# Last block of a hybrid RWKV-7 / attention layer: output rows loaded from the middle of the last gate, merge weights in pairs, raw first products, late load of x

## The chip, the cores and the metric

The kernel runs on one core of a Trainium2 chip. The time is device microseconds (us) of one execution. A core has TensorE (PE in the profile), VectorE (DVE), ScalarE (ACT), GpSimd (POOL), and SyncE (SP), which issues most of the DMAs.

## The reference, cut to what matters

One layer works on 640 tokens of width 1024 (512 latent and 128 context tokens). What the change touches is the end of the mixing part and the step behind it:

```python
u_rw, u_na, gate_rw, gate_na = jnp.split(h @ p["w_in"], IN_SPLITS, axis=-1)
o_rw, s_new = _rwkv_branch(u_rw, s0, ...)      # 8 heads of 64, a scan over the tokens in both directions
o_na = _na_latent(q, k, v, ctx_k, ctx_v, ...)  # 2-D neighbourhood attention, 8 heads of 64
merged = (jax.nn.sigmoid(gate_rw) * (o_rw @ p["w_o_rwkv"])
          + jax.nn.sigmoid(gate_na) * (o_na @ p["w_o_na"]))
x = x + g1 * (merged @ p["w_out"])
h2 = _rmsnorm(x, p["norm2_g"]) * (1.0 + sc2) + sh2
x = x + g2 * ((jax.nn.silu(h2 @ p["ffn_w1"]) * (h2 @ p["ffn_w3"])) @ p["ffn_w2"])
```

## The kernel before, in words

All tensors are float32. A product is made of three matmuls: each operand is split into a high part that the matmul takes exactly and a remainder (`split`, L185 on ACT and L186 on DVE or POOL), and hi·hi, hi·lo and lo·hi are added in PSUM. Weights are loaded 512 KB at a time into a buffer `wst` (`wdma`, L163, DMA on SP) and split by `wcast`: either ACT writes the high part (L173) and DVE subtracts (L175), or ACT writes the negated weight (L171) and an accumulating DMA that POOL issues adds the weight (L172). There are two buffers each for `wst` and for the split halves.

Attention comes first. Its output, split, is written to DRAM as `o_d`, rows 0 to 511. Then come four RWKV blocks, ct = 0 to 3, of two heads each. A block has a main part; `inv`, 30 steps on DVE that invert triangular matrices (L1250, L1254), ended by two transposes (L1263, L1265) and copies into `Rt` (L1284, L1295); `carry`, 8 sequential steps that pass a state through PE, ACT (L1327), PE, ACT (L1357), PE and DVE (L1376, tile `ZV`); and `out`, the group norm, bonus and gate (L1396 to L1412), which is spread over the next block. Three PE jobs of each block (L1145, L1148, L1173, L1185, L1196) stand at chosen steps of `inv`. Block ct = 3 leaves its output split in SBUF as `o3`.

Beside these chains runs a stream of weight units, taken in the order that the table `PRM` lists: projections (k, r, v, l), 16 gates (g0 to g15, `gate_gen`) and 16 merge units (a0 to a7: output rows 0 to 511 times `w_o`, gated with `gate_na`; b0 to b7: rows 512 to 895, gated with `gate_rw`). Their matmuls are L197 (`feat_gen`), with two PSUM buffers `fl` of 320 columns. `PRM["plan"]` gives how many of the stream's matmuls follow each step of a block. On PE, POOL, DVE and ACT the instructions of the blocks run in the order in which the code writes them; on SP a scheduler sets the order, and behind the blocks it sets that of DVE, ACT and POOL too.

The end of the stream, around which the change lies, goes like this. The last gate, g14, reads the layer's normed input `h`, whose SBUF the split output `o` takes over. So `o_load(0, 6)` (L1436, 12 DMAs of 320 KB) stands behind g14; a0 is the first reader. Each a unit (24 matmuls) loads its gate into a buffer `mx` (L1450), and DVE multiplies the PSUM result by the gate into a tile `mt` (L1464). Each b unit (18 matmuls) does the same (L1464) and adds to `mt` (L1467). Behind the blocks, `last_gen` multiplies `o3` by the last 128 rows of `w_o`: 8 chunks in two halves, 48 matmuls (L1576), each half gated (L1577), added to `mt` (L1579) and split (L1580 on ACT, L1581 on POOL). The product with `w_out` (`tok_gen`, L284; five token blocks, first 512 columns and then the other 512) is woven between. Its sums are gated with `G` (L1558) and added to `x2` (L1559), the reloaded x; that frees a PSUM bank for the other 512 columns. Loads of x (L1548, 5 of 512 KB) and G (L1553, 2 of 512 KB) go out before `last_gen`. Transposes of a small row (L1615, L1617) stand on PE between the two halves of the `w_out` product. Norm and feed-forward follow (L1718 and L284).

## Time and profile before

| | |
|---|---|
| median of 3 runs | 1191.83 us (1191.1 to 1192.4) |
| profiled execution, its own time | 1191.72 us |
| its span, first to last instruction | 1189.7 us |
| mean granted TensorE clock | 0.985 |
| PE busy | 1124.1 us (94% of the span) |
| DVE, ACT, POOL busy | 777.5, 530.5, 205.1 us |

A row of a timeline gives the start in us from the start of the span, the duration, the engine, the line, the operation and tiles, and how many instructions are joined; brackets give the idle time before it and what ended that. A window's columns are the busy us (and instructions) of PE, PE's weight loads, DVE, ACT and POOL, then the granted TensorE clock, the DMA engines' busy share and GB/s. A list of waits has the total, the count and the longest wait.

### The profile page before, as it was taken

The numbers are of one execution on the slowest core, as the hardware profiler recorded it, in microseconds if no ns is written. First come the engines' busy times: TensorE is split into PE (matmuls) and PEld (weight loads), VectorE is DVE, ScalarE is ACT, GpSimd is POOL, SyncE is SP. The second block draws the span as 40 slices with busy tenths as digits, with TensorE's granted clock in tenths as the row PEclk, the third lists the DMA queues.
The fourth block names the chain that finished last, engine by engine and source line by source line (L and its number), as shares of the span: only waits on it lengthen the run. The fifth ranks groups of instructions, "written<-read, shape, count | busy, mean of one in ns | idle before, by whom it ended". The sixth has DMA issues, their size and how long they took to land.

```text
span 1189.7 us, 26921 instructions
## 1 busy us (share of the span) xinstructions
PE 1124.1 (94%) x11160; PEld 998.3 (84%) x11160; DVE 777.5 (65%) x1630; ACT 530.5 (45%) x1053; POOL 205.1 (17%) x273
## 2 busy tenths in 40 slices
PE   6999999999999999999599799989999999999998
PEld 4688877789888988888488678889899989998997
DVE  4564455559469658836474675888568757775675
ACT  4444666554564664565133342654224422442340
POOL 1162244320111211111101250100001000000000
PEclk9999999999999999999799999999999999999999
DMA  9762767553333514433654851312312231232122
GB/s 335 265 117 84 244 216 230 191 146 98 103 93 84 153 50 104 123 93 79 200 138 110 245 218 54 107 49 79 104 57 86 89 107 54 89 100 90 59 75 103
DMA packets 61906, 149.42 MB, mean 126 GB/s; under 512 B 7732, under 2 KB 23732, under 8 KB 61784
## 3 DMA queue, kind: packets, MB, share of 16 engines
q1 hardware_dynamic: 55592, 131.56, 33.6%
q0 software_dynamic: 5328, 14.94, 6.8%
q8 instruction: 88, 1.44, 0.5%
q10 hardware_dynamic: 864, 1.20, 0.3%
q14 instruction: 34, 0.28, 0.1%
HBM read 118.41 MB, written 14.32 MB: 112 GB/s over the span
## 4 chain that ended last, share of the span: by engine, by line
PE 65%; DVE 8%; ACT 3%; DMA 2%; issue 1%; SPq 0%; ACTq 0%; DVEq 0%; POOLq 0%
PE f L1718 23%; PE acc L284 17%; PE fl L197 13%; DMA wlo<-wst 1%; DVE pr L1250 1%; PE w L1324 1%; PE w L1351 1%; DVE RL L1254 1%; PE mm L197 1%; PE w L1364 1%; PE w L1336 1%; PE w L1148 1%; DMA o<-o_d 1%; PE w L1196 1%; PE w L1126 1%
## 5 line engine op out<-in xcount | busy, mean ns | idle before, releaser
L1718 PE MATMUL f<-t,whi 128*128 128x320 f32 x640 | 141.4, 309 | 0.0
L1718 PE MATMUL f<-b,whi 128*128 128x320 f32 x608 | 136.5, 312 | 3.6 <-ACT b L185 1.8
L284 PE MATMUL acc<-whi,u 128*128 128x512 f32 (+1 forms) x448 | 136.0, 385 | 0.0
L197 PE MATMUL fl<-h,whi 128*128 128x320 f32 x704 | 126.5, 319 | 0.8 <-issue 0.8
L197 PEld LDWEIGHTS fl<-h,whi 128*128 128x128 f32 x704 | 106.1, 188 | 5.6 <-issue 0.9
L173 ACT CAST whi<-wst 128x1024 fp32r<-128x1024 f32 (+2 forms) x86 | 81.5, 953 | 64.7 <-PE acc L284 32.5
L1718 PEld LDWEIGHTS f<-t,whi 128*128 128x128 f32 x640 | 107.1, 188 | 0.0
L1718 PEld LDWEIGHTS f<-b,whi 128*128 128x128 f32 x608 | 103.0, 190 | 4.8 <-ACT b L185 2.2
L1718 PE MATMUL f<-t,wlo 128*128 128x320 f32 x320 | 98.9, 309 | 0.0
L284 PEld LDWEIGHTS acc<-whi,u 128*128 128x128 f32 x448 | 83.5, 188 | 16.7
L1718 PE MATMUL f<-b,wlo 128*128 128x320 f32 x304 | 94.7, 312 | 1.4 <-DVE wlo L1762 1.4
L1759 ACT CAST whi<-ws 128x1024 fp32r<-128x1024 f32 x40 | 42.0, 1051 | 108.7 <-PE f L1718 48.5
L1773 POOL TENSOR_TENSOR ws<-wst 128x512 f32<-128x512 f32 x20 | 28.2, 1409 | 341.3 <-DVE wlo L1762 226.7
L175 DVE TENSOR_TENSOR wlo<-wst,whi 128x1024 fp32r<-128x1024 f32 (+1 forms) x49 | 62.0, 1274 | 37.2 <-ACT whi L173 36.6
L284 PE MATMUL acc<-wlo,u 128*128 128x512 f32 (+1 forms) x224 | 86.3, 385 | 0.0
L284 PE MATMUL acc<-whi,h 128*128 128x512 f32 x240 | 78.0, 399 | 1.2 <-DVE h L398 1.1
L172 POOL DMA_DIRECT2D wlo<-wst x37 | 32.6, 881 | 232.4 <-ACT wlo L171 212.9
L1558 DVE SCALAR_TENSOR_TENSOR tt<-acc,G 128x512 f32<-128x512 f32 (+1 forms) x51 | 34.7, 681 | 50.5 <-PE acc L284 50.5
L197 PE MATMUL fl<-h,wlo 128*128 128x320 f32 x352 | 66.5, 321 | 0.0
L197 PE MATMUL fl<-o,whi 128*128 128x320 f32 x224 | 46.3, 337 | 16.8 <-DMA o<-o_d 10.0
L1759 ACT CAST whi<-wst 128x1024 fp32r<-128x1024 f32 (+1 forms) x48 | 41.3, 869 | 42.3 <-PE acc L284 37.6
L1718 PEld LDWEIGHTS f<-t,wlo 128*128 128x128 f32 x320 | 60.1, 188 | 0.0
(333 smaller groups left out, 2539.1 us busy)
## 6 DMA issues: line engine op xcount, KB each, us to landing
wst<-in_w_dram SPq DMA_DIRECT2D x66, 512.0 KB
wst<-in_w_rw_dram SPq DMA_DIRECT2D x31, 512.0 KB
wa<-in_w_ada_dram SPq DMA_DIRECT2D x24, 512.0 KB
wlo<-wst POOLq DMA_DIRECT2D x22, 512.0 KB, 4.5
f<-in_w_ada_dram SPq DMA_DIRECT2D x16, 512.0 KB
wst<-in_w_qkv_dram SPq DMA_DIRECT2D x12, 512.0 KB
o<-o_d SPq DMA_DIRECT2D x14, 320.0 KB
x<-in_xs_dram SPq DMA_DIRECT2D x8, 512.0 KB
```

Of the source, the lines that this page charges most:

```text
L172: pool.dma_start(lo[:, :n].bitcast(F32), st[:, :n], accum_op=ALU.add)
L173: act.copy(hi[:, :n], st[:, :n])
L175: dve.tensor_tensor(out=lo[:, :n], in0=st[:, :n], in1=hi[:, :n].bitcast(F32), op=ALU.subtract)
L197: pe.matmul(ps[:, :t1 - t0], w[:, a:a + 128], x[:, k0 + kt, t0:t1], start=n == 0, stop=n == 3 * nk - 1)
L284: pe.matmul(pss[i][:, a:b], lhs(x, kt, ts_), w[:, cs_], start=ki == 0 and n == 0, stop=ki == last and n == 2)
L1126: pe.matmul(t[r0:r0 + 32, 64 * i:64 * i + 64], S.BK[l // 10][own, l % 10, 0, 32 * bk:32 * bk + 32], V(AG[own, l, h, :], [[0, 2], [1, 32]], ...
L1148: pe.matmul(pr[h][hrows[h ^ i], o_], x[hrows[h], :], R_[hrows[h], l, :], start=True, stop=True)
L1196: pe.matmul(pt[h][hrows[h ^ i], o_], S.BK[l // 10][hrows[h], l % 10, i, :], idh(h), start=True, stop=True)
L1558: dve.scalar_tensor_tensor(out=tt, in0=ps[:, a:b], scalar=c, in1=G[:, g, sl], op0=ALU.mult, op1=ALU.mult)
L1718: pe.matmul(ps[:, :H2], w_[:, c_], x_[:, kt, :], start=first and kt + n == 0, stop=last and kt == 3 and n == 2, skip_group_check=more)
L1759: act.copy(r[0][:, :width], src())
L1773: eng_x(PRM["se"][i - 1]).tensor_tensor(out=o_, in0=x, in1=y, op=op)
```

## The change

Five things are changed, all in the last block and behind it.

1. The tiles that hold `h`, then `o`, then the merged sum, are cut in two halves of four row groups. The last gate is computed by a new `gate2_gen`: four row groups of both column halves, then the other four. After the first four, the first half of `h` has been read, and `o_load(0, 4)` is issued there; `o_load(4, 6)` follows where `o_load(0, 6)` stood.
2. Merge units are made in pairs: four a units of 48 matmuls (512 KB of weights each) and four b units of 36 (384 KB each). The four a units are split with POOL's DMA, the b units on DVE.
3. The a products go to `mt` raw, copied from PSUM by ACT (L1516 of the new text, where DVE's L1464 stood). A generator `gate_a` runs beside the last carry: it loads the gates (L1535) and DVE multiplies them in (L1545).
4. The last 128 rows of `w_o` are loaded into `wos` (L1599) and split (L189 on ACT, L190 on DVE) in step 0 of the last carry, no longer behind the blocks. The low part of `o3` is made by DVE, not POOL. The plan of block 3 gives a carry step 6 + 4 stream matmuls in place of 8 + 6, and has more of them in `inv`. Of the three PE jobs in `inv`, the second stands at step 8, before at step 11.
5. The pool for `x2` and `G` is opened behind the first half of the `w_out` product and takes memory that block 3 and `last_gen` used; loads of x (L1673) and G (L1678) come there. L1683 and L1684 are the former L1558 and L1559.

PE has as many instructions as before (8267 in the program's order); DVE has 1638 (1633), ACT 1009 (1012), POOL 266 (279), SP 371 (379).

SP around the loads of `o`; `wst` are pairs or single units of `w_o`, `tna_d` the gates' DRAM buffer, `o_d_80` the high and `o_d_81` the low parts. Before:

```order
L163 DMA wst_7543<-in_w_o_dram 128x512 [waits DMAHW6_49,DMAHW4_49,DMASW5_49]
L544 DMA tna_d<-fl_7413 128x320 [waits DMAHW5_49,Activation_49]
L163 DMA wst_7723<-in_w_o_dram 128x512 [waits DMAHW2_49,DMASW6_49,Activation_49]
L544 DMA tna_d<-fl_7545 128x320 [waits DMAHW7_49,Activation_49]
L1436 DMA o_7710<-o_d_81 128x640 [waits DMAHW0_49,PE_49]
L1436 DMA o_7710<-o_d_81 128x640 [waits DMAHW1_49]
L1436 DMA o_7710<-o_d_81 128x640
L1436 DMA o_7710<-o_d_81 128x640 [waits DMAHW3_49]
L1436 DMA o_7710<-o_d_81 128x640 [waits DMAHW4_49]
L1436 DMA o_7710<-o_d_81 128x640 [waits DMAHW5_49]
L1436 DMA o_7709<-o_d_80 128x640 [waits DMAHW6_49,PE_49]
L1436 DMA o_7709<-o_d_80 128x640 [waits DMAHW7_49]
```

The same place of the change:

```order
L164 DMA wst_7545<-in_w_o_dram 128x2x512 [waits DMAHW6_49,DMAHW4_49,DMASW5_49]
L559 DMA tna_d<-fl_7415 128x320 [waits DMAHW5_49,Activation_49]
L164 DMA wst_7721<-in_w_o_dram 128x2x512 [waits DMAHW2_49,DMASW6_49,Activation_49]
L1476 DMA o_7598<-o_d_81 128x640 [waits DMAHW7_49,PE_49]
L1476 DMA o_7596<-o_d_80 128x640 [waits DMAHW0_49,PE_49]
L1476 DMA o_7596<-o_d_80 128x640 [waits DMAHW1_49]
L1476 DMA o_7598<-o_d_81 128x640
L1476 DMA o_7596<-o_d_80 128x640 [waits DMAHW3_49]
L1476 DMA o_7598<-o_d_81 128x640 [waits DMAHW4_49]
L1476 DMA o_7596<-o_d_80 128x640 [waits DMAHW5_49]
L1476 DMA o_7598<-o_d_81 128x640 [waits DMAHW6_49]
```

High and low parts now alternate, and the four row groups of an a unit come first; a load of `w_o` that waits for POOL's DMA (DMASW6) still stands ahead of them.

DVE at the start of the last carry; `Rt` ends `inv`, `ZV` is the step's last operation. Before:

```order
L1295 COPY Rt<-w_8352 32x10x32 [waits Activation_49]
L1295 COPY Rt<-w_8353 32x10x32 [waits Activation_49]
L1464 SCALAR_TENSOR_TENSOR P_1091_8264<-mx_8221,fl_8334 128x320 [waits PE_49]
L1464 SCALAR_TENSOR_TENSOR kk_8402<-mx_8273,fl_8403 128x320 [waits DMAHW3_49,PE_49]
L1376 TENSOR_TENSOR ZV<-w_8429,Dt_6865 64x2x64 [waits PE_49]
L1376 TENSOR_TENSOR ZV<-w_8429,Dt_6865 64x2x64 x3
L1464 SCALAR_TENSOR_TENSOR kk_8402<-mx_8273,fl_8453 128x320 [waits PE_49]
L1376 TENSOR_TENSOR ZV<-w_8506,Dt_6865 64x2x64 [waits PE_49]
```

The change:

```order
L1333 COPY Rt<-w_8360 32x10x32 [waits Activation_49]
L1333 COPY Rt<-w_8361 32x10x32 [waits Activation_49]
L190 TENSOR_TENSOR f_1105_8468<-wos_8410,f_1104_8467 128x1024 [waits DMAHW1_49,DVE_49,Activation_49]
L1414 TENSOR_TENSOR ZV<-w_8437,Dt_6867 64x2x64 [waits PE_49]
L1414 TENSOR_TENSOR ZV<-w_8437,Dt_6867 64x2x64 x3
L1545 SCALAR_TENSOR_TENSOR mt_7723<-pre_8496,mt_7723 128x320 x2
L1545 SCALAR_TENSOR_TENSOR mt_7926<-pre_8498,mt_7926 128x320 [waits DMAHW7_49]
L1545 SCALAR_TENSOR_TENSOR mt_7926<-pre_8498,mt_7926 128x320
L1545 SCALAR_TENSOR_TENSOR mt_7977<-pre_8500,mt_7977 128x320 [waits DMAHW0_49]
L1545 SCALAR_TENSOR_TENSOR mt_7977<-pre_8500,mt_7977 128x320
L1414 TENSOR_TENSOR ZV<-w_8521,Dt_6867 64x2x64 [waits PE_49]
```

The subtraction of the last `w_o` rows now stands ahead of the first `ZV`, and six gatings stand between the first and the second.

DVE between the two halves of the `w_out` product; `acc` are the PSUM sums, `pc` the small transposes that PE makes behind the whole first half. Before:

```order
L175 TENSOR_TENSOR wlo_9379<-wst_9376,whi_9378 128x1024 [waits DVE_49,DMAHW2_49,PE_49,Activation_49]
L1558 SCALAR_TENSOR_TENSOR tt_9463<-acc_9189,G 128x512 [waits DMAHW7_49,PE_49,Pool_49]
L1559 TENSOR_TENSOR x_0_9087<-x_0_9087,tt_9463 128x512 [waits DVE_49]
L1558 SCALAR_TENSOR_TENSOR tt_9466<-acc_9190,G 128x512 [waits PE_49]
L1559 TENSOR_TENSOR x_1_9088<-x_1_9088,tt_9466 128x512 [waits DVE_49]
L1558 SCALAR_TENSOR_TENSOR tt_9469<-acc_9191,G 128x512 [waits PE_49]
L1559 TENSOR_TENSOR x_2_9089<-x_2_9089,tt_9469 128x512 [waits DVE_49]
L1558 SCALAR_TENSOR_TENSOR tt_9472<-acc_9192,G 128x512 [waits PE_49]
L1559 TENSOR_TENSOR x_3_9090<-x_3_9090,tt_9472 128x512 [waits DVE_49]
L1558 SCALAR_TENSOR_TENSOR tt_9475<-acc_9193,G 128x512 [waits DMAHW0_49,PE_49]
L1619 COPY s_9094<-pc_9439 128x16 [waits PE_49]
```

The change:

```order
L179 TENSOR_TENSOR wlo_9325<-wst_9322,whi_9324 128x1024 [waits DMAHW4_49,PE_49,Activation_49]
L1706 COPY s_9373<-pc_9402 128x16 [waits DVE_49,PE_49]
L1707 TENSOR_SCALAR m_9372<-pc_9402 128x16
L1708 TENSOR_TENSOR m_9372<-m_9372,C 128x16 [waits DVE_49]
L1683 SCALAR_TENSOR_TENSOR tt_9426<-acc_9135,G 128x512 [waits DMAHW4_49,Pool_49]
L1683 SCALAR_TENSOR_TENSOR tt_9429<-acc_9136,G 128x512
L1684 TENSOR_TENSOR x_0_9366<-x_0_9366,tt_9426 128x512 [waits DMAHW7_49,DVE_49]
L1684 TENSOR_TENSOR x_1_9367<-x_1_9367,tt_9429 128x512 [waits DMAHW0_49,DVE_49]
L1683 SCALAR_TENSOR_TENSOR tt_9432<-acc_9137,G 128x512 [waits DVE_49]
L1683 SCALAR_TENSOR_TENSOR tt_9435<-acc_9138,G 128x512 [waits DVE_49]
L1684 TENSOR_TENSOR x_2_9368<-x_2_9368,tt_9432 128x512 [waits DMAHW1_49,DVE_49]
```

The copy of `pc`, which waits for PE's transposes, now stands ahead of all the gated adds.

The core of the diff:

```diff
-     "0.0.0 16.1.0 8.1.1 9.0.0 2.1.0 8.1.1 8.1.1 ... 10.0 0.0 8.1 6.2 0.0 8.1 4.2 ..." (block 3 of the plan)
+     "0.0.0 16.1.0 8.1.1 9.0.0 2.1.0 8.1.1 13.1.1 ... 10.0 0.0 6.1 4.2 0.0 6.1 4.2 ..."
...
+    def gate2_gen(i, w, ps_, gsb, gtag):
+        ps = [ps_(), None]
+        for kts in ((0, 1), (2, 3), (4, 5), (6, 7)):
+            for hf, (a, b) in enumerate(halves):
+                if ps[hf] is None:
+                    ps[hf] = ps_()
+                for kt in kts:
+                    for n, (u, x) in enumerate(((w[0], hh), (w[0], hl), (w[1], hh))):
+                        pe.matmul(ps[hf][:, :H2], u[:, kt * 128:kt * 128 + 128], x[:, kt, a:b],
+                                  start=kt == 0 and n == 0, stop=kt == 7 and n == 2)
+                        yield
+            if kts[1] == 3:
+                o_load(0, 4)
...
-                        o_load(0, 6)
+                        o_load(4, 6)
...
-            k0, k1, src = (0, 4, tna_d) if g == "a" else (4, 7, trw_d)
-            return wdma(w_o[i][:, 128 * k0:128 * k1]), src[i]
+            k0, k1 = (0, 4) if g == "a" else (4, 7)
+            return wdma(w_o[2 * i:2 * i + 2, :, 128 * k0:128 * k1].rearrange("c p n -> p c n"))
...
+                        if g == "a":
+                            act.copy(mt[c8][:, a:b], ps[:, :b - a])
+                            copied.add((c8, a))
+                            return
...
+        def gate_a():
+            ts = []
+            def load():
+                if len(ts) < 8:
+                    ts.append(pre_t())
+                    sp.dma_start(ts[-1], tna_d[len(ts) - 1])
+            for _ in range(3):
+                load()
+            yield 0, 0
+            for c8 in range(8):
+                load()
+                for (a, b) in halves:
+                    while (c8, a) not in copied:
+                        yield 9, 9
+                    dve.scalar_tensor_tensor(out=mt[c8][:, a:b], in0=ts[c8][:, a:b], scalar=1.0, in1=mt[c8][:, a:b],
+                                             op0=ALU.add, op1=ALU.mult)
+                    yield 0, 0.45
...
-                    pg = iter(())
+                    pg = gate_a()
+                    wos = nk_t("wos", [P, 1280])
+                    sp.dma_start(V(wos[:, :], [[128, 8], [1, 128]]), w_o[:, :, 896:1024].rearrange("c p n -> p c n"))
+                    def wo_cast():
+                        wo.extend(f5()[:, 0:1024].bitcast(F32R) for _ in range(2))
+                        split(wo[0], wo[1], wos[:, 0:1024])
+                    later(wo_cast, (0.95, 1.1), 12)
...
-    wo = wload(w_o[:, :, 896:1024].rearrange("c p n -> p c n"))
...
-    nstack.close()
-    xpool = open_pool(ctx, "xpool")
...
     hs.close()
+    nstack.close()
+    xpool = open_pool(ctx, "xpool")
```

172 lines of the change are left out of this document (102 added, 70 removed).

## Prediction

> **What bounds the kernel now.** First the page: PE's busy share. Then PE's waits and the windows of the last block, to see where PE is not busy. Then the timelines of the engines waited for.
>
> ```profile
> PE 1124.1 (94%) x11160; PEld 998.3 (84%) x11160; DVE 777.5 (65%) x1630; ACT 530.5 (45%) x1053; POOL 205.1 (17%) x273
> ```
>
> ```profile
> 570.00:580.00 10.00, 6.07 (x21) 5.12 (x22) 2.08 (x8) 0.92 (x1) 0.00 (x0) 0.50 0.82 287
> 660.00:670.00 10.00, 8.41 (x55) 7.59 (x55) 4.97 (x11) 4.00 (x10) 3.79 (x4) 1.00 0.94 260
> 670.00:680.00 10.00, 6.56 (x38) 5.76 (x38) 6.74 (x12) 3.52 (x5) 2.47 (x2) 0.99 0.79 233
> 680.00:690.00 10.00, 9.62 (x39) 8.70 (x40) 10.00 (x18) 2.80 (x7) 5.37 (x7) 0.67 1.01 408
> sum 180.00, PE 154.45 PEld 135.11 DVE 109.88 ACT 59.09 POOL 41.05; mean PE 8.58 PEld 7.51 DVE 6.10 ACT 3.28 POOL 2.28
> ```
>
> ```profile
> PE fl L197 <- DMA o<-o_d: 10.0, 1, 10.0
> PE fl L197 <- DVE mt L1464: 4.7, 1, 4.7
> PE fl L1576 <- ACT o L185: 3.1, 1, 3.1
> PE fl L197 <- DVE P L1464: 2.1, 2, 1.5
> PE acc L284 <- DVE wlo L175: 2.0, 1, 2.0
> ```
>
> PE is busy in 94% of the span, so little can be won outside its gaps. The windows' sum covers 550 to 730: PE is busy 154.45 of 180 us, idle 25.6. That is the ceiling, for PE's number of instructions does not change. Five waits name the gaps: the load of `o`, twice a PSUM buffer that DVE frees, the split of `o3`, and a weight's low part. The profiled run took 1191.72 us, 0.11 below the median of 1191.83, with a span of 1189.7; I sum against 1191.72 and take the 2.0 outside the span as unchanged.
>
> **A. Loads of `o` from the middle of the last gate.**
>
> ```profile
> 557.13 0.86 POOL L172 DMA_DIRECT2D wlo<-wst  x1 [0.36 <-issue]
> 560.57 0.33 SPq L163 DMA_DIRECT2D wst<-in_w_o_dram  x1
> 562.20 8.15 SPq L1436 DMA_DIRECT2D o<-o_d  x12
> 573.93 3.07 PE L197 MATMUL fl<-o,whi 128*128 128x320 f32 x7 [10.04 <-DMA o<-o_d]
> wlo<-wst POOLq DMA_DIRECT2D x22, 512.0 KB, 4.5
> ```
>
> PE ends the gate at 563.9 and waits 10.0, to 573.9. But SP issues the first load at 562.20 already, because the load of `w_o` ahead of it waits until POOL's DMA of 557.13 has landed (560.57, 3.4 us for 256 KB). In the change the same wait stands ahead, and that DMA is a pair of 512 KB, which takes 4.5 us by the last row: 561.6, then the loads at about 562.1. So issuing from the middle of the gate moves nothing; SP is held elsewhere. What is won comes from the order. Before, six low parts land first and the fourth high part is the tenth of twelve; now the fourth row group is complete with the eighth. Two loads of 320 KB at 408 GB/s (680 to 690, where the DMA engines were full) are 1.6 us. A weight load twice as large in front takes 0.6 back. Products of the first three groups now lie beside the landing of the fourth; of the seven matmuls behind 573.93 (3.07 us at a granted clock of 0.50) about four leave the path, 0.8 us more at least. I take **1.8**, between 0 (the larger transfers eat it) and 3.5.
>
> [...]
>
> The gate in two halves holds both `fl` buffers from its start. The second is freed by ACT's tanh of g15, perhaps 1 us late; PE would wait for `o` behind it anyway, so 0. Without that cover it costs the 1 us.
>
> **B. DVE rid of the a gatings in `inv`.**
>
> ```profile
> 579.43 0.49 DVE L1464 SCALAR_TENSOR_TENSOR mt<-mx,fl 128x320 f32<-128x320 f32 x1
> 593.47 0.47 DVE L1464 SCALAR_TENSOR_TENSOR mt<-mx,fl 128x320 f32<-128x320 f32 x1
> 593.87 0.46 DVE L1250 TENSOR_TENSOR pr<-RL 128x112 f32<-128x112 f32 x2
> 601.94 0.68 DVE L175 TENSOR_TENSOR wlo<-wst,whi 128x512 fp32r<-128x512 f32 x1
> 609.58 0.49 DVE L1464 SCALAR_TENSOR_TENSOR P<-mx,fl 128x320 f32<-128x320 f32 x1 [3.45 <-PE fl L197]
> 621.18 0.49 DVE L1464 SCALAR_TENSOR_TENSOR P<-mx,fl 128x320 f32<-128x320 f32 x1
> 562.01 1.19 PE L197 MATMUL fl<-h,wlo 128*128 128x320 f32 x7
> 563.04 0.70 PE L1094 MATMUL w<-bv,K 128*128 128x320 f32 x2
> 662.27 0.43 ACT L1397 COPY out<-w 128x320 f32<-128x320 f32 x1 [2.38 <-PE w L1396]
> ```
>
> DVE is the chain here: `inv` cannot end before its last step. Twelve gatings stand between 579.43 and the carry's start, the last at 621.18, each pushing the next instruction back by 0.40 (593.47 to 593.87): 4.8. The subtraction at 601.94 goes to POOL (0.6), but one of 768 columns now stands before the copies into `Rt`; between 0.68 for 512 and 1.23 for 1024 that is an estimated 0.9. The gating at 609.58 waited 3.45 us for PE, with both transposes of `inv` behind it: gone too. 4.8 + 0.6 − 0.9 + 3.45 = 8.0. Against it, the stretch gets 25 more stream matmuls (counted in the order), 0.147 us each (seven from 562.01 to 563.04): 3.7, which PE pays from its own waits for DVE (4.7 and 2.1), because ACT now frees the buffers at 0.43 a copy. But ACT's copies stand in its written order behind the split of the last output, so not all of that wait goes. Between 3 (PE keeps its 4.7 wait) and 8.0 I take **6.0**, nearer to the upper end because DVE, not PE, is the chain.
>
> **C. The carry.**
>
> ```profile
> 623.83 0.86 ACT L1357 COPY ZV<-w 64x128 f32<-64x128 f32 x4 [0.78 <-PE w L1351]
> 625.81 1.25 DVE L1376 TENSOR_TENSOR ZV<-w,Dt 64x128 f32<-64x128 f32 x4 [1.01 <-PE w L1364]
> 646.11 0.27 ACT L1327 COPY x<-w 128x128 f32<-128x128 f32 x1 [2.00 <-PE w L1324]
> 650.41 0.27 ACT L1327 COPY x<-w 128x128 f32<-128x128 f32 x1 [1.51 <-PE w L1324]
> 648.67 0.61 DVE L1376 TENSOR_TENSOR ZV<-w,Dt 64x128 f32<-64x128 f32 x2 [2.43 <-PE w L1364]
> 641.22 0.49 DVE L1467 TENSOR_TENSOR mt<-mt,mx 128x320 f32<-128x320 f32 x1
> 670.21 0.38 SPq L163 DMA_DIRECT2D wst<-in_w_o_dram  x1
> 674.72 1.05 ACT L173 CAST whi<-wst 128x1024 fp32r<-128x1024 f32 x1 [4.01 <-PE fl L197]
> 675.80 1.23 DVE L175 TENSOR_TENSOR wlo<-wst,whi 128x1024 fp32r<-128x1024 f32 x1 [2.12 <-ACT whi L173]
> ```
>
> A step takes 4.30 us (646.11 to 650.41). PE's queue has 28 stream matmuls fewer in the eight steps: 28 × 0.147 = 4.1 won. Two things are added. First, the split of the last `w_o` rows: ACT's cast (1.05) comes behind its `ZV` copies, which ended at 624.7, and behind one copy of 0.43; DVE's subtraction (1.23) stands ahead of the first `ZV`, which would end its wait at 627.4 rather than 625.81: 1.6 lost, and the whole step chain is behind it. The load must be there: before, the same load went out at 670.21 and its cast began at 674.72, so it lands within 4.5 us; issued when PE has read the tile that it overwrites, at about 619, it is in time. If SP is held, up to 5 is lost. Second, sixteen gatings of 0.49, two per step. DVE idles 2.4 us ahead of `ZV` at 648.67 and a step becomes 0.5 shorter, so two gatings mostly fit; but up to six (2.9) stand between two `ZV`s, and two weight subtractions of 768 columns come to DVE from POOL. I charge 1.2, between 0 and 4. C is 4.1 − 1.6 − 1.2 = **1.3**, from −3 to +4.
>
> The gating from PSUM takes 0.47 (593.47) or 0.49 (579.43), the add from SBUF alone 0.49 (641.22), all 128x320, so I count a gating from SBUF like one from PSUM. [...]
>
> **D. From the carry to `last_gen`.**
>
> ```profile
> 679.03 0.53 PE L1576 MATMUL fl<-o,whi 128*128 128x320 f32 x2 [3.09 <-ACT o L185]
> ```
>
> `last_gen` starts at 679.03. PE idles 1.6 + 3.4 = 5.0 us in the two windows from 660 to 680. ACT's cast of the `w_o` rows (674.72) waited 4.0 us for PE to free a weight buffer, and the split of `o3`, for which PE then waits 3.1, stood behind it. Both casts and POOL's share leave. The norm's chain stays, so a last 1.0 of waiting too: **4.0**, between 2 and 5.
>
> **E. `last_gen`.** DVE is busy 10.00 of 10 us from 680 to 690, and has the same gatings, adds and weight subtractions after; two of the latter now stand between the gatings, which removes PE's 2.0 and delays the gatings as much. 0, from −2 to +2.
>
> **F. x late.**
>
> ```profile
> 698.51 5.59 POOL L1581 TENSOR_TENSOR m<-tr,m 128x320 fp32r<-128x320 f32 x4 [1.00 <-ACT m L1580]
> 715.42 0.69 DVE L1558 SCALAR_TENSOR_TENSOR tt<-acc,G 128x512 f32<-128x512 f32 x1 [6.09 <-PE acc L284]
> 720.70 1.15 PE L1617 MATMUL pc<-K,arow 2*128 2x2 f32 x16
> 722.58 0.62 PE L284 MATMUL acc<-whi,m 128*128 128x512 f32 x2
> 723.27 0.61 PE L284 MATMUL acc<-whi,m 128*128 128x512 f32 x2
> ```
>
> Before, gated adds start at 715.42, as soon as the first sums are done, and the other half follows the transposes (720.70 + 1.15) without a wait. Now DVE first copies `pc`, that is, waits for the transposes, to 721.85, and does three small operations, to about 722.2. The first gated sum is then out of PSUM at 722.9: PE starts 1.1 late. The third follows two gatings and two adds: 722.2 + 5 × 0.69 = 725.6, where PE, taking 0.69 per token block (722.58 to 723.27), wants it at 724.3: 1.3 more. Loads of x and G wait until POOL's last subtraction has ended (704.1); 7 × 524 KB at 408 GB/s is 9.0 us, so G lands near 716, hidden by 6 us. **−2.5**, from −1 to −6.
>
> **Sum.** 1.8 + 6.0 + 1.3 + 4.0 + 0 − 2.5 = 10.6; 1191.72 − 10.6 = 1181.1, forecast **1181.0**.
>
> **Rivals.**
>
> *The carry is held by DVE and ACT, and `o` comes no earlier* (A 0 instead of 1.8, C −3 instead of 1.3): 6.1 less, 4.5 of gain, **1187.2**. For it: the six gatings between two `ZV`s, SP's wait. Against: the 2.4 us of idle in a step.
>
> *The chains give everything* (A 3.5, B 8.0, C 2.7, D 4.5, F −1.5): 17.2, **1174.5**. For it: 25.6 us of idle PE. Against: each chain has other waits next.
>
> *The change does not do what it says*: the loads are not earlier, ACT's copies free PSUM as late as DVE did, and gains in the tail are eaten by x (A 0, B 3, C −2, D 2, F −2.5): 0.5, **1191.2**.
>
> *Slower, by late x.* If the memory of x and G is free only when the first half of the product has ended (720.7), 0.6 for the small rows, 9.0 to 12.8 of transfer (408 GB/s, or the 287 of 570 to 580) and some 2 of landing put G at 732 to 736, and the other half starts 11 to 15 us late, with 1.3 from DVE's order on top: up to 16.4 against the 13.1 won before it, **1195.0**. It decides if G lands later than about 733 on this clock. Against: the weights of that product are not in the pools that x takes.
>
> **How the numbers follow.** Forecast 0.50 (1177.5 to 1185), held carry 0.22 (to 1189), everything 0.13 (down to 1173), no effect 0.05, late x 0.10. A measurement of this kernel tells about 0.2% (2.4 us) from no change. So faster 0.85, same 0.05, slower 0.10. The range reaches over the held carry and the best case: 1173.0 to 1190.0; no effect and late x are left out.
>
> **What would show it.** A: the wait for `o` ends near 571 to 572, first load near 562. B: no wait for L1516, the transposes of `inv` near 602 to 605 (now 610 to 613). C: a step of 3.7 to 3.9 us, the first one 1.6 longer. D: `last_gen` near 666. F: a wait of PE for DVE's L1683 of 2 to 3 us. I am wrong if PE waits for DVE in the carry by more than 4 us, if the wait for `o` stays at 10, or if G is what L1683 waits for.

## Result and the profile after

The changed kernel takes **1182.15 us** (median of six runs, 1180.3 to 1184.24) against 1192.95 for the kernel before, run beside it (six runs, 1191.1 to 1194.95): ratio 0.9914, 95% interval 0.9899 to 0.9929, a gain of 8.5 to 12 us. The forecast was 1181.0 us. The profiled execution took 1182.22 us with a span of 1180.4; before it was 1191.72 and 1189.7.

The page of the changed kernel, PE's waits from 540 to 770, and four windows, one of the wait for `o` and three of `inv`:

```profile
PE 1123.0 (95%) x11160; PEld 995.3 (84%) x11160; DVE 777.8 (66%) x1635; ACT 531.6 (45%) x1050; POOL 192.1 (16%) x260
```

```profile
PE fl L201 <- DMA o<-o_d: 7.7, 7, 2.9
PE fl L1644 <- DVE pre L1645: 2.5, 1, 2.5
PE acc L288 <- DVE tt L1683: 1.9, 2, 1.2
...
PE fl L201 <- DVE mx L1520: 1.4, 2, 0.8
```

```profile
570.00:580.00 10.00, 5.53 (x16) 3.90 (x16) 0.62 (x2) 0.00 (x0) 0.00 (x0) 0.53 1.03 339
...
590.00:600.00 10.00, 9.98 (x68) 9.72 (x67) 9.99 (x47) 4.98 (x9) 1.21 (x2) 1.00 0.74 218
600.00:610.00 10.00, 9.76 (x236) 9.45 (x237) 9.37 (x31) 4.82 (x10) 0.86 (x1) 1.00 0.52 134
610.00:620.00 10.00, 9.98 (x242) 8.90 (x241) 5.46 (x12) 4.41 (x12) 0.00 (x0) 1.00 0.30 93
```

PE does the same work; what went are waits. The 4.7 and 2.1 for a gating that frees `fl`, the 3.1 for the split of `o3` and the 2.0 for a weight's low part are gone. The wait for `o` is 7.7 in place of 10.0; 2.5 for the first gating of `last_gen` and 1.9 for the gated sums are new. PE is now nearly full in `inv`, and DVE with it up to 610.

To compare kernels stage by stage I count from one row, GpSimd's DMA that opens the stretch: its start varies between executions of nearly identical programs by up to 4 us (543.86 to 547.81 in the runs below), all of it work that the change doesn't touch. In the changed kernel and in the one before:

```profile
546.13 0.86 POOL L176 DMA_DIRECT2D wlo<-wst  x1 [14.01 <-ACT wlo L175]
```

```profile
545.30 0.86 POOL L172 DMA_DIRECT2D wlo<-wst  x1 [14.02 <-ACT wlo L171]
```

The table gives what lies from the start of that row to: the first low-part product of `o` (PE), the end of the second transpose of `inv` (DVE), the first step of the last carry (ACT's first copy into `x`), the copy that ends that carry (ACT), and the transposes into `pc` (PE). The next column is from `pc` to the end of the span. The last two are the ratio to the kernel before, measured beside it, and its interval; the medians of before in the three sets of runs were 1191.37, 1191.39 and 1191.22.

| kernel | `o` low | inv ends | carry | carry ends | pc | pc to end | median us | ratio | 95% |
|---|---|---|---|---|---|---|---|---|---|
| before | 32.8 | 67.9 | 77.4 | 114.0 | 175.4 | 469.0 | | 1 | |
| the change | 31.1 | 61.4 | 72.4 | 104.7 | 163.8 | 470.5 | 1182.15 | 0.9914 | 0.9899 to 0.9929 |
| gate_end | 31.2 | 61.4 | 72.4 | 104.7 | 163.8 | 470.5 | 1181.59 | 0.9918 | 0.9904 to 0.9931 |
| no_mid | 33.8 | 63.0 | 74.0 | 106.3 | 165.8 | 471.8 | 1186.01 | 0.9951 | 0.9939 to 0.9963 |
| gated_a | 30.9 | 70.5 | 81.0 | 112.8 | 171.9 | 470.6 | 1191.45 | 1.0004 | 0.9993 to 1.0016 |
| raw_alone | 32.4 | 59.8 | 69.3 | 105.2 | 169.5 | 469.1 | 1188.11 | 0.9968 | 0.9956 to 0.9981 |
| plan_old | 31.4 | 59.9 | 67.9 | 104.5 | 164.1 | 470.6 | 1182.15 | 0.9923 | 0.9910 to 0.9937 |
| head_only | 31.1 | 61.4 | 72.4 | 104.2 | 164.8 | 468.9 | 1180.59 | 0.9910 | 0.9896 to 0.9923 |
| adds_first | 30.8 | 61.2 | 72.2 | 104.4 | 163.6 | 468.2 | 1180.72 | 0.9907 | 0.9890 to 0.9924 |
| cast_late | 31.0 | 60.8 | 71.7 | 104.0 | 164.3 | 472.3 | 1183.50 | 0.9933 | 0.9920 to 0.9945 |
| o_first | 24.9 | 54.6 | 65.6 | 97.8 | 157.0 | 470.6 | 1177.37 | 0.9886 | 0.9871 to 0.9901 |
| o_first_gated | 25.8 | 63.7 | 74.7 | 106.5 | 166.0 | 471.9 | 1187.39 | 0.9963 | 0.9949 to 0.9978 |
| best_a | 26.1 | 57.1 | 68.0 | 100.3 | 159.4 | 468.2 | 1173.81 | 0.9855 | 0.9842 to 0.9868 |
| best_b | 26.0 | 56.0 | 67.0 | 99.3 | 158.5 | 468.8 | 1176.03 | 0.9867 | 0.9853 to 0.9881 |

The six columns of stages come from one profiled execution each, and executions of the same code differ: up to `pc` the change, gate_end and adds_first agree within 0.5 us, but o_first, best_a and best_b, whose edits differ only behind the carry, lie up to 2.5 apart before it, and no_mid's 471.8 behind `pc` is 1.3 above the change's with the same code. In both cases PE's granted clock differs between the executions: from 570 to 580 it is 0.83 in o_first and best_b and 0.69 in best_a; in the first 8 us behind `pc` it is 0.79 in no_mid and 1.00 in the change (the last section has finer rows). A median may lie 1 to 3 us off what the execution shows (the profiled executions of raw_alone and o_first were the shortest of theirs). The kernel before took 1192.95 us beside the change and 1191.22 to 1191.39 beside the others, so a median set against the change's has 1.6 us of play. By the ratios, o_first is 3.3 us below the change, best_a 7.0, adds_first 0.8 and head_only 0.5; plan_old is 1.1 above it and no_mid 4.4.

The copy at "carry ends" is late in the kernel before. ACT splits weights ahead of it there, and waits 1.32 us for PE to do so, while PE's last product of the carry, which the copy reads, is done at 657.2 (656.78 + 0.45):

```profile
656.78 0.45 PE L1381 MATMUL w<-TG,ZV 128*64 128x64 f32 x8
658.35 0.53 ACT L171 ACTIVATE wlo<-wst 128x384 fp32r<-128x384 f32 x1 [1.32 <-PE fl L197]
659.30 0.59 ACT L1386 COPY out<-w 128x512 f32<-128x512 f32 x1
```

In the change that product starts at 650.30 and the copy follows at 650.80.

```profile
650.30 0.45 PE L1419 MATMUL w<-TG,ZV 128*64 128x64 f32 x8
```

### The profile page after: what moved, and what is told of

Same layout as the page of the kernel before. It is cut to its first block, busy times and chain, and to the rows that moved or that the text cites. A ratio compares the mean times of both kernels' runs of the same rounds, so it can differ in the third digit from the quotient of the medians.

```text
span 1180.4 us, 26871 instructions
## 1 busy us (share of the span) xinstructions
PE 1123.0 (95%) x11160; PEld 995.3 (84%) x11160; DVE 777.8 (66%) x1635; ACT 531.6 (45%) x1050; POOL 192.1 (16%) x260
## 3 DMA queue, kind: packets, MB, share of 16 engines
q1 hardware_dynamic: 55464, 131.56, 34.1%
## 4 chain that ended last, share of the span: by engine, by line
PE 62%; DVE 9%; ACT 3%; issue 3%; DMA 1%; SPq 0%; POOL 0%; DVEq 0%; ACTq 0%; POOLq 0%
PE f L1805 21%; PE acc L288 16%; PE fl L201 12%; PE w L1362 1%; PE w L1389 1%; DVE pr L1288 1%; PE w L1402 1%; DMA o<-o_d 1%; PE w L1374 1%; PE mm L201 1%; PE w L1186 1%; DVE RL L1292 1%; PE w L1380 1%; PE w L1419 1%; PE w L1234 1%
## 5 line engine op out<-in xcount | busy, mean ns | idle before, releaser
L201 PE MATMUL fl<-h,whi 128*128 128x320 f32 x672 | 121.2, 320 | 1.3 <-issue 1.3
L177 ACT CAST whi<-wst 128x1024 fp32r<-128x1024 f32 (+1 forms) x77 | 79.2, 1033 | 63.6 <-PE acc L288 43.0
L201 PEld LDWEIGHTS fl<-h,whi 128*128 128x128 f32 x672 | 101.4, 188 | 6.1 <-issue 1.4
L201 PE MATMUL fl<-h,wlo 128*128 128x320 f32 x336 | 63.4, 321 | 0.0
L1683 DVE SCALAR_TENSOR_TENSOR tt<-acc,G 128x512 f32<-128x512 f32 (+1 forms) x51 | 34.5, 679 | 42.8 <-PE acc L288 42.7
L1846 ACT CAST whi<-wst 128x1024 fp32r<-128x1024 f32 (+1 forms) x48 | 41.4, 870 | 42.3 <-PE acc L288 37.6
L1805 PEld LDWEIGHTS f<-b,wlo 128*128 128x128 f32 x304 | 57.5, 189 | 2.5 <-DVE wlo L1849 2.5
L1849 DVE TENSOR_TENSOR wlo<-ws,whi 128x1024 fp32r<-128x1024 f32 x40 | 54.9, 1372 | 6.3 <-ACT whi L1846 6.3
```

What stands on the lines that cost most here:

```text
L177: act.copy(hi[:, :n], st[:, :n])
L201: pe.matmul(ps[:, :t1 - t0], w[:, a:a + 128], x[:, k0 + kt, t0:t1], start=n == 0, stop=n == 3 * nk - 1)
L1683: dve.scalar_tensor_tensor(out=tt, in0=ps[:, a:b], scalar=c, in1=G[:, g, sl], op0=ALU.mult, op1=ALU.mult)
L1805: pe.matmul(ps[:, :H2], w_[:, c_], x_[:, kt, :], start=first and kt + n == 0, stop=last and kt == 3 and n == 2, skip_group_check=more)
L1846: act.copy(r[0][:, :width], src())
L1849: dve.tensor_tensor(out=r[1][:, :width], in0=src(), in1=r[0][:, :width].bitcast(F32), op=ALU.subtract)
```

## Experiments

The runs gate_end, no_mid, gated_a, raw_alone, plan_old and head_only ask which part carries the gain, the others what is still left beside them. Part 2, the merge units in pairs, has no run of its own. Each run starts from the changed kernel unless it says otherwise.

### Part 1: where the loads of `o` are issued

gate_end:

```diff
-            if kts[1] == 3:
+            if kts[1] == 7:
                 o_load(0, 4)
```

> The changed kernel with o_load(0, 4) issued behind the last gate instead of in its middle; all else as changed. Theory (a load of w_o ahead of them holds SP to 562.5, and behind the gate the loads would wait for PE's last read of h at 565.8): the first load of o goes out 2.5 to 3 us later than 563.0, the carry starts 2 to 3 us later than 618.5, the time rises by 2 to 3 us. Rival (only the order of the loads counts, because the DMA engines are full behind 570): the carry starts within 0.7 us of 618.5 and the time stays.

1181.59 us; the loads are issued 16.8 us after the opening row, as in the change (16.9). The rival held. The first half of the tile is free when the gate's fourth row group is done, whatever the line at which the load is written.

no_mid:

```diff
-    ... lg=14, ...
+    ... lg=-1, ...
-                        o_load(4, 6)
+                        o_load(0, 6)
```

> The changed kernel with part 1 undone as far as the order of the loads goes: the last gate is made as before, one column half after the other, and all loads of o stand behind it; the tiles stay cut in two. Theory (part 1 is worth the 1.8 us of term A, since the last group of the first four lands only 1 to 2 us earlier): first low-part product of o 1.5 to 2 us later after the start of the stretch (31.1 us in the change), time 1183 to 1184.5. Rival (the loads in the middle overlap the gate's second half and spare TensorE a stall with its lower granted clock): 4 us or more, 1185.5 or above. Second rival (SyncE's held load decides alone): below 0.7, 1181.5 to 1182.5.

1186.01 us, 3.9 above the change; its trace has 2.0 of it before `pc` and 1.3 behind it, where no edit was made. The first low-part product is 2.7 later. Its loads go out 1.0 later than in the change (17.9 against 16.9 us), because a store of the gate stands ahead of them again. PE waits once for 12.1, as the kernel before does, in place of seven waits of 7.7 together: the parts that the first products need land together and late. So 1.0 of the 2.7 goes with the later issue, and the other 1.7 is put down to the order high, low, high, low, which the halved gate brings about; no run changes the order alone. By the time it is the rival's range that holds, by the trace up to `pc` the theory's.

o_first (the third load of a `w_o` pair is held behind the first eight loads of `o`):

```diff
+            if g == "a" and i == 2:
+                with tc.issue_after(first_o[0].ins):
+                    return wdma(w_o[4:6, :, 128 * k0:128 * k1].rearrange("c p n -> p c n"))
             return wdma(
```

> The changed kernel, but the third load of a pair of w_o rows, which waits for GpSimd's accumulating DMA, is issued behind the first eight loads of o instead of ahead of them. Theory (SyncE held behind that load is what delays o): the loads go out when TensorE has read the first half of h, about 3 us earlier, the first product of o starts 2 to 3 us earlier, and the carry's start follows by 1 to 3 us: 1178.6 to 1180.6 us. Rival (the way ahead of inv's VectorE chain, not the loads of o, sets the carry's start): the first product comes earlier, the carry's start by less than 0.5 us, time 1181 to 1182.

1177.37 us, 4.8 below the change by the medians and 3.3 by the ratios, and 6.8 less up to `pc` in its trace. The theory had 1.5 to 3.5 for the time and 1 to 3 for the carry's start; its mechanism holds, and its size was at least reached. At the carry's start o_first is 6.8 ahead of the change, and best_a and best_b, which hold the same edit, 4.4 and 5.4, so 6.8 is the luckiest of three executions. SP and PE of the change, then of o_first (start, duration, operation, count, wait):

```profile
562.53 0.38 SPq L164 DMA_DIRECT2D wst<-in_w_o_dram  x1
563.01 4.73 SPq L1476 DMA_DIRECT2D o<-o_d  x8
```

```profile
568.74 0.53 PE L201 MATMUL fl<-o,whi 128*128 128x320 f32 x2 [2.91 <-DMA o<-o_d]
...
577.22 1.27 PE L201 MATMUL fl<-o,wlo 128*128 128x320 f32 x4
```

```profile
560.74 5.33 SPq L1479 DMA_DIRECT2D o<-o_d  x8
566.18 0.60 SPq L164 DMA_DIRECT2D wst<-in_w_o_dram  x1
```

```profile
567.04 0.53 PE L201 MATMUL fl<-o,whi 128*128 128x320 f32 x2 [0.15 <-DMA o<-o_d]
...
570.97 0.41 PE L201 MATMUL fl<-o,whi 128*128 128x320 f32 x1 [0.52 <-DMA o<-o_d]
...
572.08 0.77 PE L201 MATMUL fl<-o,wlo 128*128 128x320 f32 x4
```

The loads go out 3.3 us sooner after the opening row (560.74 − 547.18 = 13.6 against 563.01 − 546.13 = 16.9), and from the first load to the first low-part product it takes 11.3 in place of 14.2, with the 512 KB pair no longer in front. PE's wait for `o` falls from 7.7 to 2.4 (3.3 in best_a). How the 2.9 divides between the pair's own transfer and PE's clock was not tried.

### Part 3: raw a products

gated_a (part 3 undone: DVE gates the a products from PSUM in `inv`, no gatings in the carry):

```diff
-                            act.copy(mt[c8][:, a:b], ps[:, :b - a])
-                            copied.add((c8, a))
+                            dve.scalar_tensor_tensor(out=mt[c8][:, a:b], in0=t[:, a:b], scalar=1.0,
+                                                     in1=ps[:, :b - a], op0=ALU.add, op1=ALU.mult)
...
-                    later(rest, (0.45, 0) if g == "a" else (0, 1.0))
+                    later(rest, (0, 0.5) if g == "a" else (0, 1.0))
...
-                    pg = gate_a()
+                    pg = iter(())
```

> The changed kernel with the a products gated by DVE from PSUM inside inv again (gates loaded into the two mx buffers, no gate_a in the carry). Theory (DVE is the chain of inv): the transposes and the carry's start move back by 3 to 5 us, PE waits for DVE to free a PSUM buffer again by 3 us or more, and the carry gets no shorter, as its last operation of a step waits for PE anyway; time up by 3 to 5 us. Rival (PE is the chain of inv and the gatings cost as much in the carry): start of the carry within 1 us, carry 1 to 3 us shorter, time the same or lower.

1191.45 us, ratio 1.0004: the whole gain is gone with this part, about twice the 3 to 5 us that the theory gave it. `inv` ends 9.1 us later. PE's waits in gated_a:

```profile
PE fl L201 <- DVE mt L1518: 2.8, 1, 2.8
...
PE fl L201 <- DVE P L1518: 2.2, 2, 1.6
```

and DVE at the end of `inv`, where a gating waits for PE and both transposes queue behind it:

```profile
612.86 0.49 DVE L1518 SCALAR_TENSOR_TENSOR P<-mx,fl 128x320 f32<-128x320 f32 x1 [3.29 <-PE fl L201]
613.26 2.08 DVE L1301 STREAM_TRANSPOSE f<-RL 128x1024 f32<-128x1024 f32 x1
```

Behind the wait of 2.8, from 590.2 to 593.0, PE's granted clock is 0.69 and then 0.50, which the theory left out. Windows of gated_a (PE's busy time is the second number, the granted clock the third from the end):

```profile
592.00:594.00 2.00, 1.01 (x4) 1.01 (x5) 2.00 (x8) 0.00 (x0) 0.00 (x0) 0.69 0.70 210
594.00:596.00 2.00, 2.00 (x9) 2.00 (x9) 2.00 (x11) 0.00 (x0) 0.00 (x0) 0.50 0.82 246
```

In the change the clock is 1.00 in both windows. In gated_a twelve matmuls of `o` behind the wait take 3.29 us (from the start at 592.99 to the next at 596.28), the twelve after them 1.76 (to 598.04): 1.5 us more. How much of this reaches the end of `inv` was not separated.

raw_alone (part 3 alone, put into the kernel before):

```diff
+                    if g == "a":
+                        act.copy(mt[c8][:, a:b], ps[:, :b - a])
+                        copied.add((c8, a))
+                        return
...
-                    pg = iter(())
+                    pg = gate_a()
```

> Part 3 alone, put into the kernel before: the a products go to mt raw by ScalarE's copies and are gated in the last carry; loads of o, single weight units, plan, w_o's last rows and x stay as before. Theory (the gain is ScalarE freeing the fl buffers, so that neither VectorE's chain nor TensorE's queue in inv waits for a gating): the end of inv comes 6 to 9 us earlier as it does between gated_a and the change (9.1 there), the carry keeps its 4.3 us step with up to 1.2 us of gatings on top, and last_gen waits as before: gain 5 to 8, 1183.5 to 1186.5 us. Rival (the raw copies only pay together with the other parts, because the plan puts 24 matmuls more into inv that need the freed buffers): with the old plan TensorE had no more work for these gaps, and the gain is 0 to 3, 1188.5 to 1191.5.

1188.11 us, a gain of 3.3 by the medians and 2.3 to 5.2 by the interval. The medians lie between the two ranges. Up to the carry it does what the theory said: 8.1 us earlier than before at the end of `inv` and at the carry's start. At PE's last product of the carry it is 6.8 earlier (650.74 − 546.06 = 104.7 against 656.78 − 545.30 = 111.5), chiefly because the first step grew from 5.30 to 6.46. From there to the first gating of `last_gen` it loses another 1.3 (26.1 against 24.8). PE waits there for ACT's split of `o3`, 3.3 us against 3.1 before; the cast ahead of that split, which before waited for PE, now waits for a load of `w_o`:

```profile
670.01 1.05 ACT L173 CAST whi<-wst 128x1024 fp32r<-128x1024 f32 x1 [5.29 <-DMA wst<-in_w_o_dram]
```

So the gain goes with part 3, but put in alone it gives about a third of it. Which of the other parts keeps the rest is not shown: the plan loses nothing when it is undone, nor do the early split and the late x together (below), and the pairs were not tried.

o_first_gated (both edits):

> The changed kernel with part 3 undone (gatings from PSUM in inv, as in gated_a) and with the third w_o load behind the first eight loads of o (as in o_first). Theory (TensorE's wait for o and VectorE's gatings are in series, because inv's chain needs jobs that stand in TensorE's queue behind the products of o): the gain of o_first stays, 5 to 7 us below gated_a, 1184.5 to 1186.5. Rival (VectorE's chain of gatings runs beside the wait for o, and the later of the two sets the end of inv): 0 to 2 us below gated_a, 1189.5 to 1191.5.

The edits are those of o_first and gated_a. 1187.39 us, with nine runs from 1183.89 to 1190.35; 4.1 below gated_a by the medians, 5.9 up to `pc` in the traces. The gain of o_first stays, so the waits for `o` and the gatings are in series, as the theory said, though the median gives a little less than its 5 to 7.

### Part 4: the plan and the last `w_o` rows

plan_old (the plan of block 3 and its jobs as before):

```diff
-        ("10.0 0.0 6.1 4.2 0.0 6.1 4.2 ..."
+        ("10.0 0.0 8.1 6.2 0.0 8.1 4.2 ..."
```

> The changed kernel with the stream's plan and the places of the three TensorE jobs of block 3 as they were before (8 + 6 stream matmuls a carry step, 24 fewer in inv); all else changed. Theory (the carry is bound by TensorE's queue, 28 matmuls of 0.147 us): the step goes from 3.72 back to about 4.3 us and the carry's end comes 4 us later; in inv TensorE has 3.5 us less, of which VectorE's chain gives back 0 to 2: 1183.5 to 1186 us. Rival (the step is VectorE's and ScalarE's chain, and the shorter step comes from elsewhere): the step stays below 3.9 and the time within 1 us of the change, 1180.7 to 1182.7.

1182.15 us: no difference. The time is the rival's, but the step is the theory's: the carry takes 36.6 us in place of 32.3. It starts 4.5 earlier, because PE has 25 matmuls less ahead of it (25 × 0.147 = 3.7; the rest may lie in the places of the jobs, which this run moves too). ACT's step in plan_old and in the change:

```profile
640.29 0.27 ACT L1365 COPY x<-w 128x128 f32<-128x128 f32 x1 [2.96 <-PE w L1362]
644.60 0.27 ACT L1365 COPY x<-w 128x128 f32<-128x128 f32 x1 [2.04 <-PE w L1362]
```

```profile
618.53 0.37 ACT L1365 COPY x<-w 128x256 f32<-128x256 f32 x1 [1.84 <-PE w L1362]
625.00 0.37 ACT L1365 COPY x<-w 128x256 f32<-128x256 f32 x1 [2.75 <-PE w L1362]
...
641.09 0.27 ACT L1365 COPY x<-w 128x128 f32<-128x128 f32 x1 [2.36 <-PE w L1362]
644.81 0.27 ACT L1365 COPY x<-w 128x128 f32<-128x128 f32 x1 [1.51 <-PE w L1362]
650.80 0.59 ACT L1424 COPY out<-w 128x512 f32<-128x512 f32 x1 [0.91 <-PE w L1419]
```

A step takes 4.31 against 3.72. The plan moves matmuls between two stretches in both of which PE is nearly full (8.97, 10.00 and 9.96 of 10 us in the change from 620 to 650).

head_only (last `w_o` rows loaded and split behind the blocks again, x and G loaded early again):

```diff
-                    later(wo_cast, (0.95, 1.1), 12)
...
     mh, ml = hilo("m")
+    wo = wload(w_o[:, :, 896:1024].rearrange("c p n -> p c n"))
```

> The changed kernel with parts 4 and 5 undone: the last rows of w_o are loaded and split behind the blocks, and x and G are loaded ahead of last_gen, as before. Theory by the sum of the prediction corrected by the trace of after: the first carry step is 1.2 us shorter, the stretch from the carry's last copy to last_gen is 2 to 4 us longer, the wait for the gated adds (1.9) goes; together 0 to 1 us slower. Rival (the tail is where the gain came from): 4 us slower or more.

1180.59 us, where the theory had 0 to 1 more than the change: the split in the carry and part 5 give nothing together. The first carry step is 6.0 us in place of 6.5, `last_gen` loses 0.9 again (18.7 from the carry's end to its first matmul, against 17.9), and the wait for the gated sums is gone.

### Part 5, and what is left

adds_first (the copies of `pc` behind the gated adds):

```diff
-    dve.tensor_copy(s2, V(pc[:, :], [[2, 8], [1, 2]]))
 ...
     for i in range(5):
         add_gated(pss[i], i, 0, 0.5)
+    tc.keep_in_program_order(dve.tensor_copy(s2, V(pc[:, :], [[2, 8], [1, 2]])))
```

> The changed kernel with DVE's copies of pc put behind the gated adds of the first half. Theory (F: PE waits because DVE stands at the copy of pc, while G has landed long before): PE's wait for DVE L1683 of 1.9 us goes, the time falls by 1.5 to 2 us. Rival (x and G land late): the adds now wait for a DMA, PE waits as long as before or longer, and the time stays.

1180.72 us, 1.4 below the change by the medians and 0.8 by the ratios, with overlapping intervals; the theory had 1.5 to 2. PE's wait of 1.9 is gone, and `pc` to the end takes 468.2 in place of 470.5, which is the theory's size.

cast_late (the first split for the other half of the `w_out` product held back):

```diff
+        with tc.issue_after(lastm[0].ins):
+            c4 = wcast(c4)
```

> The changed kernel, but the split of the first weight of w_out's other half is held until ScalarE has done last_gen's last cast, so that VectorE does not do its 1.2 us subtraction ahead of last_gen's first gating. Theory (between the carry and last_gen VectorE is the chain): the first gating of last_gen starts 1.2 us earlier and the time falls by 1.0 to 1.4, to 1180.2 to 1180.6 us. Rival (VectorE is busy through all of last_gen, so the subtraction only moves): the first gating is earlier, but the small transposes behind the product are not, time 1181 to 1182.

1183.50 us, above the rival's 1181 to 1182 as well. Its mechanism held: `last_gen`'s first gating is 1.8 us earlier (124.1 against 125.9; 0.7 of it was there at the carry's end already), `pc` 0.5 later. The subtraction now falls among `last_gen`'s gatings, and two of this size take 1.90 (677.11) and 1.85 there, longer than the 1.22 that one takes ahead of them. DVE of cast_late:

```profile
666.86 1.22 DVE L179 TENSOR_TENSOR wlo<-wst,whi 128x1024 fp32r<-128x1024 f32 x1
...
680.79 1.85 DVE L179 TENSOR_TENSOR wlo<-wst,whi 128x1024 fp32r<-128x1024 f32 x1
```

best_a (o_first and adds_first) and best_b (also one split moved from DVE to GpSimd's DMA):

```diff
+        c4 = wload(w_out[4], pool)
```

> o_first and adds_first together: the held w_o load behind the first eight loads of o, and the gated adds ahead of the copies of pc. Theory (two separate waits of TensorE, 5.3 us of waiting for o with its slower clock, and 1.9 for the gated sums): 1.0 to 1.9 us below o_first, 1175.5 to 1176.5. Rival (the transposes' copies come late for the norm instead): same as o_first, 1177 to 1178.

> best_a, and the first weight of w_out's other half is split with GpSimd's accumulating DMA in place of VectorE's subtraction, which stands ahead of last_gen's first gating. Theory (VectorE is the chain from the carry through last_gen, busy 10 of 10 us, so an instruction taken off it shortens the whole): 1.0 to 1.5 us below best_a. Rival (in cast_late, with the subtraction moved behind, the transposes came no earlier, because TensorE and the later weight splits take over): within 0.5 us of best_a.

best_a takes **1173.81 us**, ratio 0.9855 (0.9842 to 0.9868), the fastest here: 8.3 below the change (7.0 by the ratios) and 17.4 below the kernel before. It is 3.6 below o_first, more than the theory's 1.0 to 1.9. The traces show the 2.4 of adds_first behind `pc` (468.2 in place of 470.6), but its execution loses as much again up to `pc` (159.4 against 157.0) in the same code, so from the opening row on the two are equal there. best_b, 1176.03, is no faster than best_a; its 2.2 above it are more than its rival's 0.5, but from the opening row to the end their traces agree within 0.4.

## Why the prediction was right, and where its terms were off

The total held, and so did the likeliest case: 10.6 forecast, 9.5 in the profiled executions. The measured terms below add up to 10.2; 0.8 of it is lost ahead of the opening row (546.13 against 545.30), which the change doesn't touch.

**A, 1.8.** Measured 1.7 (32.8 to 31.1 us). The place of issue moves nothing as long as the order stays (gate_end), and without the halved gate 2.7 goes (no_mid). The heavier weight load in front takes back 1.0 of that: no_mid is 1.0 later than the kernel before, because its load of `w_o` goes out 16.9 after the opening row in place of 15.3. But the bound of 3.5 was too low for what the place hides. I named SP's held load and then priced only its hold; taken out of the way it gives 4.4 to 6.8 at the carry's start in three traces (best_a, best_b, o_first).

**B, 6.0.** This is the term that was over-sized. A and B together bring the carry 5.0 us forward, not 7.8, so B is 3.3. The step that failed is "PE pays from its own waits": the 8.0 that DVE is rid of is right (raw_alone, which has the gatings' part of it, 4.8 + 3.45, shows 8.1), but the 25 stream matmuls added to the stretch are paid in full. plan_old takes them out and its carry starts 4.5 earlier. The windows of the change show why: PE is busy 9.98, 9.76 and 9.98 of 10 us, so what DVE no longer does, PE does. Two waits on the way, in the change's DVE timeline, show the next links: the split of 768 columns, estimated at 0.9, took 0.96 and waited for ACT's cast, and `Rt` waited for ACT too.

```profile
610.92 0.96 DVE L179 TENSOR_TENSOR wlo<-wst,whi 128x768 fp32r<-128x768 f32 x1 [0.76 <-ACT whi L177]
...
616.41 0.89 DVE L1333 COPY Rt<-w 32x320 f32<-32x320 f32 x2 [0.97 <-ACT Rt L1333]
```

**C, 1.3.** Up to ACT's closing copy the carry became 4.4 us shorter (36.63 to 32.27), but 2.0 of this is not the step chain: it is ACT's work on weights ahead of the copy, shown below the table, which the prediction did not price. Up to PE's last product the carry went from 34.1 to 31.8, so 2.3 was won where 1.3 was forecast. The plan's matmuls came in whole: with them back, plan_old takes 36.1 (650.97 − 614.84) in place of 31.8, 4.4 for the 4.1 forecast. The two charges of 1.6 and 1.2 were too high: plan_old, with split and gatings, takes 2.0 more than the kernel before, 1.2 in the first step (6.47 against 5.30) and 0.8 in the fourth (5.14 against 4.31). DVE in the first two steps of the change:

```profile
621.96 1.22 DVE L190 TENSOR_TENSOR f<-wos,f 128x1024 fp32r<-128x1024 f32 x1 [4.66 <-ACT f L189]
...
624.49 2.50 DVE L1545 SCALAR_TENSOR_TENSOR mt<-pre,mt 128x320 f32<-128x320 f32 x6
628.24 0.61 DVE L1414 TENSOR_TENSOR ZV<-w,Dt 64x128 f32<-64x128 f32 x2 [1.25 <-PE w L1402]
```

Six gatings take 2.50 and `ZV` still waits 1.25 for PE, so behind the first step DVE has room: the other steps are as long in the change as in gated_a, which has no gatings there (4.93 and then 3.72). In the first step, split and gatings cost about 0.45 each when one is taken out: 6.03 in gated_a (no gatings) and 6.02 in head_only (no split), against 6.47 with both.

**D, 4.0.** Measured 1.9: from the carry's closing copy to `last_gen`'s first matmul it was 679.03 − 659.30 = 19.7 us before, and is 668.67 − 650.80 = 17.9 now. The casts left, but in their place PE waits for DVE's gatings of the b units (1.4), which the prediction did not name as next, and the weight splits of the last `w_o` rows are worth 0.9 of it (head_only). With the 2.0 ahead of the copy, the stretch from PE's last product of the carry gave 3.9, but those 2.0 are of other casts than the ones named.

**E, 0 and F, −2.5.** Measured +0.4 and −1.5. Of F, 0.8 is put down to the clock, an estimate: adds_first, with the order of adds of the kernel before, takes 468.2 behind `pc` against 469.0, and PE's granted clock is 0.79 from 752 to 760 in the kernel before, and 1.00 at the same place behind `pc` in the change and in adds_first. Against adds_first, which differs by the order of the adds alone, the change pays 2.3 (470.5 against 468.2), so 2.5 was nearly right. G is loaded at 698.6 and hides, as said; the wait for L1683 is 1.9. The two rows of F in the change, DVE's and PE's:

```profile
711.10 0.17 DVE L1706 COPY s<-pc 128x16 f32<-128x16 f32 x1 [12.55 <-PE pc L1704]
...
711.49 1.28 DVE L1683 SCALAR_TENSOR_TENSOR tt<-acc,G 128x512 f32<-128x512 f32 x2
```

```profile
712.22 0.73 PE L288 MATMUL acc<-whi,m 128*128 128x512 f32 x2 [1.16 <-DVE tt L1683]
```

B was 2.7 too high and D 2.1; C was 3.1 too low, F 1.0 and E 0.4. That the total came within 1.1 of the forecast is in good part luck: the errors have opposite signs, and 2.0 of C come from work of ACT that no term had.

Of the rivals, the held carry failed (C came out positive), and late x failed with G in time; its "some 2 of landing" was an estimate. In the change the load of x issued at 694.15 (512 KB) moves its last bytes at about 697.2, 3.0 us later, of which 1.3 is the transfer at 408 GB/s. "Everything" was not reached by the change, but best_a shows that its 1174.5 was to be had, more than half of the step to it in A and the rest in F, not in the chains it summed.

Open: what the pairs of part 2 are worth, which part keeps what part 3 wins, and what decides whether PE's clock falls.

## What to carry to other kernels

Work moved from one stretch to the next is worth what the bound engine has free there: count it on both sides, and if PE is full in both, book zero. When a row names what holds a queue, price the case in which it is taken out of the way before setting a bound; here a 512 KB load that could wait stood ahead of 2.6 MB that could not, and moving it was worth more than any other single edit tried on top of the change. A part is judged by taking it out as well as by putting it in alone: by the medians part 3 costs 9.3 taken out of the change and gives 3.3 put into the kernel before.
